# A two-layer decoder step on one core: low parts of the normalized input moved from VectorE to GpSimd, weight splits and norm sums reordered

## The chip, the cores and the metric

One Trainium2 chip, one core of it. The metric is the time of one execution in microseconds, as the device reports it; the median of several runs is given. The engines are called as in the profile: PE (TensorE), DVE (VectorE), ACT (ScalarE), POOL (GpSimd), SP (the engine whose queue issues most loads).

## The reference

One inference step of two layers, on a prompt of 256 tokens and 8 sampled tokens (264 columns in all), width 1024, float32. Layer 0 mixes tokens by a gated short convolution, layer 1 by block-sparse attention with 8 heads of 128. Each layer has one input projection to 4096 columns, a mixer, a gate and one output projection, and ends in a layer norm of the residual:

```
q, k, v, z = jnp.split(x @ w_in, 4, axis=-1)          # layer 1
yp = (o.reshape(Bp, Tp, D_MODEL) * jax.nn.silu(z)) @ w_out_attn[j]
xp = _layernorm(DN_ALPHA * xp + yp, ln_g[i], ln_b[i])  # both layers
```

So the normalized output of layer 0, called x1 here, is the input of layer 1's projection. That is the place of the change.

## The kernel before

**Products.** Activations lie feature by token: 8 blocks of 128 features, each 264 columns wide. A weight is taken in slabs: slab n holds 128 output features as 8 blocks of 128x128. Slabs 0 to 31 are layer 0's input projection, 32 to 39 its output projection, 40 to 71 layer 1's input projection (q in 40 to 47, then k, v, z) and 72 to 79 the output projection. To keep float32 accuracy at the speed of a rounded format, each operand is split into a rounded high part and a low part, which is the difference; per block k, `mm` (L136 to L138) issues three products: high by high, low weight by high, high weight by low. A slab is 24 products into one PSUM accumulator. There are three accumulators under the tag "acc", used in turn, so slab n writes the one that slab n - 3 wrote and has to wait until that has been read.

**Splits of weights.** `load` (L112) brings a slab by a DMA from SP, `hi` (L124) rounds it on ACT, `lo` (L129) takes the difference on DVE. Where each is issued is written by hand: `hi_slot` and `lo_slot` give the slab during which it is issued, and behind `lo` of a slab the load of the slab four places on is issued, into the buffer that has just come free.

**Order.** All engines run their instructions in program order. Before the products of slab n, `begin(n)` runs the work hooked to n by `at(n, phase, ...)`, phase by phase: dma, pe, s0, hi, lo, s1a, s1b, s1, s1c, and then, by `split_late`, hi3 and lo3. Within a phase the order is that of registration. For slabs 40 and 41 this is written out by hand (from L1027 on), with `split_late` called apart.

**The norm between the layers.** In slabs 33 to 39, `evac` adds the projection to the residual in `xf`, `square` squares it on ACT, and `sums` adds values and squares over the eight blocks on POOL, into the tiles sr and q (264 wide). `last_sums` adds block 7 on DVE. `stats_mm` (L335) multiplies the two with a column of 1/1024 (of -1/1024 for the mean), each in four products of 66 tokens that go to four groups of 32 partitions (L341); it is issued behind blocks 0 to 3 of slab 40. `stats` then gets the negative mean and the reciprocal of the deviation: a copy and a square on ACT (L349, L350), a subtraction on DVE (L351), a root on ACT (L352), a reciprocal on DVE (L353). Sixteen small copies spread these to the tile nr (L357): five on DVE, four on POOL, seven on ACT, those of ACT behind the rounding of slab 45.

**Slabs 40 to 46** don't wait for the norm: they multiply the residual, scaled by the norm's gain, and are mended afterwards. `u_evac` (L580 to L583) does this for one slab on DVE: a copy of two columns, a product that adds the accumulator (L582, its last reader) and a product with the reciprocal of the deviation (L583). `u_fin` adds the bias on ACT (L586) and POOL copies the 8 sampled columns (L587).

**Slabs 47 to 71** multiply x1. `x1_norm` subtracts the mean and scales, in two passes on DVE (L839, L840). `x1_affine` applies gain and bias on ACT (L844) and rounds (L845, the high part). `x1_low` (L848) takes the low part on DVE. These are hooked two blocks at a time: norms of blocks 0 and 1 in slab 41, 2 and 3 in 42, 4 and 5 in 43, 6 and 7 in 44; low parts 0 and 1 in slab 43, 2 and 3 in 45, 4 to 7 in 46.

**In the middle of slab 47**, behind its block 3, PE takes 64 products of the sampled tokens' scores (L745). They read the tile zq, which DVE fills in slab 46 (shuffle and rotation from L622 on, then L736) from POOL's copies of heads 0 to 3.

The lines around the change:

```
for n, norm, low in ((42, (2, 3), ()), (43, (4, 5), (0, 1)), (44, (6, 7), ()),
                     (45, (), (2, 3)), (46, (), (4, 5, 6, 7))):
    for m in norm:
        at(n, "s1", x1_norm, m)
        at(n, "s1", x1_affine, m)
    for m in low:
        at(n, "s1", x1_low, m)
```

Of the kernel before, what the change touches and what calls it, by code (L numbers as in the profile page):

```python
# [10 lines left out]
F32 = mybir.dt.float32  # L11
# [3 lines left out]
AF = mybir.ActivationFunctionType  # L15
ALU = mybir.AluOpType
# [5 lines left out]
N = T + B  # L22
# [27 lines left out]
def build(tc, a):  # L50
    nc = tc.nc
    pe, act, dve, pool, sp = nc.tensor, nc.scalar, nc.vector, nc.gpsimd, nc.sync

    with ExitStack() as top:
# [7 lines left out]
        def acc_full():  # L62
            return psp.tile([128, 512], F32, tag="acc", bufs=3, name="acc")

        def acc_tile():
            return acc_full()[:, 0:N + 2]

        def att_tile(nm):
            return psp.tile([128, 512], F32, tag="att", bufs=3, name=nm)
# [20 lines left out]
        xf = cp.tile([128, NB, N], F32, name="xf")  # L90
# [3 lines left out]
        pair = [[t[:, :, 4:N + 6] for t in ts] for ts in rows_of]  # L94
# [36 lines left out]
        def mm(acc, n, mv, ks, first=True, last=True):  # L131
            mh, ml = mv
            w = acc.shape[-1]
            for k in ks:
                wh, wl = his[n][:, k, :], los[n][:, k, :]
                pe.matmul(acc, wh, mh[:, k, 0:w], start=first and k == ks[0], stop=False)  # L136
                pe.matmul(acc, wl, mh[:, k, 0:w], start=False, stop=False)  # L137
                pe.matmul(acc, wh, ml[:, k, 0:w], start=False, stop=last and k == ks[-1])  # L138
# [4 lines left out]
        def at(n, phase, f, *args):  # L143
            hooks.setdefault((n, phase), []).append(lambda: f(*args))

        def run(n, phase):
            for f in hooks.pop((n, phase), []):
# [2 lines left out]
        hi_slot = {4: 3, 5: 3, 6: 3, 7: 4, 8: 4, 9: 5, 10: 5, 11: 6, 38: 33, 39: 34, 40: 22, 41: 24, 42: 26,  # L150
                   43: 36, 44: 37, 45: 40, 46: 41, 47: 43, 48: 45, 49: 46, 50: 47, 51: 48, 52: 48, 53: 49,
                   54: 51, 55: 52, 56: 53, 57: 53, 58: 54, 65: 61, 66: 62, 67: 63, 68: 63, 78: 74}
        lo_slot = {4: 3, 5: 3, 6: 3, 7: 4, 8: 5, 9: 5, 45: 40, 46: 42, 47: 44, 51: 49, 52: 49,
                   53: 50, 54: 51, 55: 52, 56: 53, 57: 54, 58: 54, 61: 58, 62: 59, 63: 60, 64: 61, 65: 61, 66: 62, 67: 63, 39: 34}

        order = []
# [4 lines left out]
        for i, n in enumerate(order):  # L161
            hs = hi_slot.get(n, n - 5)
            late = "3" if 45 <= n < 50 else ""
            at(hs, "hi" + late, hi, n)
            ls = lo_slot.get(n, hs + 1)
            if n in (61, 62, 65):
                late = "4"
            elif ls in (56, 57, 58):
                late = "3"
            elif n == 46:  # L170
                late = ""
            at(ls, "lo" + late, lo, n)
            if i + 4 < len(order):
                at(ls, "lo" + late, load, order[i + 4])

        def begin(n, end=True):
            for ph in ("dma", "pe", "s0", "hi", "lo", "s1a", "s1b", "s1", "s1c"):
                run(n, ph)
            if end:
                split_late(n)  # L180
# [75 lines left out]
        onem = cp.tile([128, 2, 32], F32, name="onem")  # L256
# [28 lines left out]
        G = N // 4  # L285
# [4 lines left out]
        class Norm:  # L290
# [23 lines left out]

            def square(self, m):
                if m == 0:
                    self.q = self.t("q")
                    act.activation(self.q, xf[:, 0], AF.Square)
                    return
                self.sq[m] = lnp.tile([128, N], F32, tag="sqm", bufs=2, name=f"sqm{m}{self.gi}")  # L320
                act.activation(self.sq[m], xf[:, m], AF.Square)

            def sums(self, m):
                if m == 1:
                    self.sr = self.t("sr")
                    pool.tensor_tensor(self.sr, xf[:, 0], xf[:, 1], ALU.add)
                else:
                    pool.tensor_tensor(self.sr, self.sr, xf[:, m], ALU.add)
                pool.tensor_tensor(self.q, self.q, self.sq[m], ALU.add)
# [3 lines left out]
                dve.tensor_add(self.q, self.q, self.sq[7])  # L333

            def stats_mm(self):  # L335
                self.mean = att_tile("ln0")
                self.e2 = att_tile("ln1")

                def acc(p, w, src, first, last):
                    for j in range(4):  # L340
                        pe.matmul(p[32 * j:32 * j + 32, 0:G], w, src[:, G * j:G * j + G],  # L341
                                  start=first, stop=last)
                acc(self.mean, onem[:, 0], self.sr, True, True)
                acc(self.e2, onem[:, 1], self.q, True, True)

            def stats(self):
                self.st = self.t("st", 2 * G)
                var = self.t("var", G)
                act.copy(self.st[:, 0:G], self.mean[:, 0:G])  # L349
                act.activation(var, self.mean[:, 0:G], AF.Square)  # L350
                dve.tensor_sub(var, self.e2[:, 0:G], var)  # L351
                act.activation(var, var, AF.Sqrt, bias=epst)  # L352
                dve.reciprocal(self.st[:, G:2 * G], var)  # L353

# [136 lines left out]
        for n in range(4, 32):  # L491
# [3 lines left out]
            acc = acc_tile()[:, 0:N]  # L495
# [39 lines left out]
        with tc.tile_pool(name="l1", bufs=1) as p1, ExitStack() as late_pool:  # L535
            x1 = pair[1]
# [305 lines left out]
            def x1_affine(m):  # L842
                c = xf[:, m]
                act.activation(c, c, AF.Identity, bias=ln.bcol(m), scale=ln.gcol(m))  # L844
                act.copy(x1[0][:, m, 0:N], c)  # L845

            def x1_low(m):
                dve.tensor_sub(x1[1][:, m, 0:N], xf[:, m], x1[0].bitcast(F32)[:, m, 0:N])  # L848

            S = 40  # L850

# [34 lines left out]
            for h in range(8):  # L886
                n = S + 16 + h
# [138 lines left out]

            ac2 = [acc_tile() for _ in range(2)]  # L1027
            begin(40, False)
            mm(ac2[0], 40, pair[0], range(0, 4), last=False)
            ln.stats_mm()  # L1030
            ln.stats()
            ln.nr = lnp.tile([128, 4, 2 * G], F32, name="nr")
# [2 lines left out]
            ln.spread(pool.tensor_copy, [(j, 1) for j in range(4)])  # L1035
            split_late(40)
            ln.spread(act.copy, [(j, 3) for j in range(4)] + [(j, 2) for j in range(3)])
            mm(ac2[0], 40, pair[0], range(4, 7), first=False, last=False)
            begin(41, False)
            mm(ac2[1], 41, pair[0], range(0, 3), last=False)  # L1040
            for m in (0, 1):
# [1 line left out]
            split_late(41)  # L1043
            for m in (0, 1):
                x1_affine(m)
            mm(ac2[1], 41, pair[0], range(3, 7), first=False, last=False)
            for i in range(2):
                mm(ac2[i], 40 + i, pair[0], range(7, 8), first=False)
                at(42, "s0", u_evac, i, ac2[i])
                at(42, "s1", u_fin, i)  # L1050
            for n, norm, low in ((42, (2, 3), ()), (43, (4, 5), (0, 1)), (44, (6, 7), ()),
                                 (45, (), (2, 3)), (46, (), (4, 5, 6, 7))):
                for m in norm:
                    at(n, "s1", x1_norm, m)
                    at(n, "s1", x1_affine, m)
                for m in low:
                    at(n, "s1", x1_low, m)
            for i in range(2, 32):
                n = S + i
                begin(n)  # L1060
                mv = pair[0] if i < NU else x1
                acc = acc_tile()
                if i >= NU:
                    acc = acc[:, 0:N]
# [43 lines left out]
            last = [acc_full(), att_tile("c1b")]  # L1108
# [11 lines left out]
            for k in range(8):  # L1120
                for c in range(2):
                    for j in range(4):
                        pe.matmul(ps[32 * j:32 * j + 32], gs[:, c, k, :],  # L1123
                                  wide(raws, k)[:, 256 * j + 128 * c:256 * j + 128 * c + 128],
                                  start=k == 0 and c == 0, stop=False)
# [93 lines left out]
```

## Time and profile before

| | |
|---|---|
| median of 3 runs | 276.52 us (276.19 to 276.76) |
| the profiled execution | 276.77 us, of which the span of the program 275.0 us |
| PE busy | 270.2 us (98%) |
| DVE busy | 203.5 us (74%) |
| ACT busy | 170.6 us (62%) |
| POOL busy | 64.9 us (24%) |
| granted clock of PE | 1.0 |

How to read it: the profile is of one execution. Times are from the start of its span. In a timeline, a row gives the start and the duration in us, the engine, the line of the kernel (L129), the operation, the tile written and those read, the shapes and how many instructions are merged; in brackets the engine's idle time before it, and what ended that. Shares of busy time are means over the whole span; the place of the change is the stretch from 120 to 150 us. Records of one engine can overlap a little, since an instruction starts before the one ahead has fully ended.

### The profile page before, as it was taken

To read this page: it belongs to the slowest core of one execution; us is meant where nothing else is said; L and a number is where in the kernel's file an instruction comes from. 1 tells how busy PE (TensorE), PEld (TensorE's weight loads), DVE (VectorE), ACT (ScalarE), POOL (GpSimd) and SP (SyncE) were. 2 spreads that over 40 slices of the span, in tenths; PEclk is the share of its full clock that TensorE was granted. 3 is DMA by queue.
4 is the path that set the end of the run, shared out by engine and by line. 5 is a ranking of instruction groups with operands and counts; after the bars stand their busy time and mean duration, and the time that the engine had idled before them with its cause. 6 is when DMAs were issued, how large, how long until landed. Compare 5 with 4: busy or idle time off the path is not lost.

```text
span 275.0 us, 6282 instructions
## 1 busy us (share of the span) xinstructions
PE 270.2 (98%) x2307; PEld 254.7 (93%) x2307; DVE 203.5 (74%) x415; ACT 170.6 (62%) x348; POOL 64.9 (24%) x129
## 2 busy tenths in 40 slices
PE   8999999999999999999999999999999999999994
PEld 5999999999999999999999997999959996998883
DVE  3888966655775857979999839799857484994745
ACT  4786554453655628549686665888746854599302
POOL 1121532020110101961312365721100030000122
PEclk9999999999999999999999999999999999999999
DMA  7976879999785875142223999997989955782012
GB/s 245 401 274 223 281 286 333 396 360 377 245 266 197 283 227 189 56 147 76 80 76 99 343 401 357 337 393 233 354 308 348 391 183 174 219 272 75 1 76 88
DMA packets 24336, 66.48 MB, mean 242 GB/s; under 512 B 3058, under 2 KB 6898, under 8 KB 24178
## 3 DMA queue, kind: packets, MB, share of 16 engines
q1 hardware_dynamic: 23874, 65.69, 68.0%
q8 instruction: 18, 0.29, 0.4%
q10 hardware_dynamic: 432, 0.39, 0.4%
q14 instruction: 12, 0.10, 0.1%
HBM read 61.67 MB, written 3.35 MB: 236 GB/s over the span
## 4 chain that ended last, share of the span: by engine, by line
PE 98%; ACT 0%; DVE 0%; issue 0%
PE acc L136 24%; PE acc L137 24%; PE acc L138 24%; PE c L1010 4%; PE acc L472 3%; PE sd L745 3%; PE dps L796 3%; PE c1b L1010 2%; PE acc L1010 2%; PE acc L475 1%; PE so L1123 1%; PE warmp L80 1%; PE s L679 1%; PE o L717 1%; PE pt L707 1%; PE s L677 1%
## 5 line engine op out<-in xcount | busy, mean ns | idle before, releaser
L124 ACT CAST hi<-raw 128x1024 fp32r<-128x1024 f32 x76 | 79.0, 1049 | 34.3 <-DMA raw<-w 15.7
L129 DVE TENSOR_TENSOR lo<-raw,hi 128x1024 fp32r<-128x1024 f32 x76 | 92.7, 1230 | 7.1 <-ACT hi L124 3.9
L136 PE MATMUL acc<-m0h,hi 128*128 128x264 f32 (+1 forms) x280 | 79.4, 283 | 0.0
L138 PE MATMUL acc<-m0l,hi 128*128 128x264 f32 (+1 forms) x280 | 79.2, 283 | 0.0
L137 PE MATMUL acc<-m0h,lo 128*128 128x264 f32 (+1 forms) x280 | 79.2, 283 | 0.0
L136 PE MATMUL acc<-m1h,hi 128*128 128x264 f32 x264 | 76.4, 289 | 0.0
L138 PE MATMUL acc<-m1l,hi 128*128 128x264 f32 x264 | 74.6, 282 | 0.0
L137 PE MATMUL acc<-m1h,lo 128*128 128x264 f32 x264 | 74.5, 282 | 0.0
L137 PEld LDWEIGHTS acc<-m0h,lo 128*128 128x128 f32 x280 | 52.8, 189 | 0.0
L136 PEld LDWEIGHTS acc<-m0h,hi 128*128 128x128 f32 x280 | 52.6, 188 | 0.1
L138 PEld LDWEIGHTS acc<-m0l,hi 128*128 128x128 f32 x280 | 52.7, 188 | 0.0
L136 PEld LDWEIGHTS acc<-m1h,hi 128*128 128x128 f32 x264 | 49.6, 188 | 1.7 <-issue 0.8
L137 PEld LDWEIGHTS acc<-m1h,lo 128*128 128x128 f32 x264 | 49.8, 189 | 0.0
L138 PEld LDWEIGHTS acc<-m1l,hi 128*128 128x128 f32 x264 | 49.5, 188 | 0.0
L428 POOL COPY uo<-up 128x10 f32<-128x10 f32 x8 | 9.0, 1122 | 64.3 <-DVE up L427 58.5
L635 POOL COPY vs<-vh 128x8 f32<-128x8 f32 x8 | 3.0, 375 | 33.1 <-ACT vh L634 33.1
L688 DVE CUSTOM_DVE_ANT_0 P<-s,cst 128x128 f32<-128x128 f32 (+1 forms) x16 | 5.1, 355 | 6.2 <-PE s L679 6.2
L436 DVE SCALAR_TENSOR_TENSOR t<-up,cst,t 128x256 f32<-128x256 f32 x8 | 3.9, 483 | 6.9 <-ACT t L435 6.9
L825 POOL COPY zs<-z 128x8 f32<-128x8 f32 x8 | 3.0, 378 | 24.4 <-ACT z L824 24.4
L824 ACT ACTIVATE z<-acc 128x264 f32<-128x264 f32 x8 | 3.1, 386 | 9.0 <-PE acc L138 9.0
L952 ACT ACTIVATE zq<-raw 128x1024 f32<-128x1024 f32 x8 | 8.5, 1061 | 0.1
L427 DVE TENSOR_TENSOR up<-acc,h 128x264 f32<-128x264 f32 x8 | 3.4, 430 | 6.9 <-PE acc L138 6.9
(226 smaller groups left out, 446.5 us busy)
## 6 DMA issues: line engine op xcount, KB each, us to landing
raw<-w SPq DMA_DIRECT2D x76, 512.0 KB, 4.5
kv<-kc SPq DMA_DIRECT2D x32, 256.0 KB, 6.2
kv<-vc SPq DMA_DIRECT2D x16, 512.0 KB, 6.4
first<-first SPq DMA_DIRECT2D x6, 388.0 KB, 7.1
v_o<-vh SPq DMA_DIRECT2D x8, 132.0 KB, 5.5
xf<-kall SPq DMA_DIRECT2D x16, 64.0 KB, 2.6
kall<-gb SPq DMA_DIRECT2D x1, 1024.0 KB, 6.1
k_o<-kall SPq DMA_DIRECT2D x6, 132.0 KB, 5.4
```

Of the source, the lines that this page charges most:

```text
L124: act.copy(his[n][sl], raws[n][sl])
L129: dve.tensor_sub(los[n][sl], raws[n][sl], his[n].bitcast(F32)[sl])
L136: pe.matmul(acc, wh, mh[:, k, 0:w], start=first and k == ks[0], stop=False)
L137: pe.matmul(acc, wl, mh[:, k, 0:w], start=False, stop=False)
L138: pe.matmul(acc, wh, ml[:, k, 0:w], start=False, stop=last and k == ks[-1])
L428: pool.tensor_copy(uo[:, f], up[:, T:N + 2])
L472: pe.matmul(accs[s], wh, (mh, ml)[c], start=k == 0 and c == 0, stop=False)
L688: dve.tensor_tensor_reduce(out=P[sl], in0=s_ps[h][sl], in1=mask[sl], scale=-SCALE, scalar=3e38, op0=ALU.add, op1=ALU.min, accum_out=mx[:, ...
L745: pe.matmul(s[32 * j:32 * j + 16, 0:256], zq[:, o:o + 16], kt, start=step == 0 and i == 0, stop=step == 3 and i == 3)
L796: pe.matmul(dps[0][32 * j:32 * j + 32, 512 * c:512 * c + 512], pm[b2][pg][:, j, :], kv_tiles[step, j][:, 512 * c:512 * c + 512], start=ste ...
L952: act.activation(od, wide(raws, k), AF.Copy, accum_out=wsum[:, k:k + 1])
L1010: pe.matmul(acc, g[m][:, k, t], wide(d, k)[:, c0:c1], start=k == 0 and i == 0, stop=k == 7 and i == 2)
```

## The change

It has four parts, all between slab 40 and slab 47.

- **Norm sums.** The sums sr and q become the two halves of one tile, and `stats_mm` makes four products of 2 x 66 columns instead of twice four of 66. They go behind block 4 of slab 40 instead of block 3. The mean comes out positive and ACT turns its sign in L349.
- **Splits.** `lo` of slab 45 moves from slot 40 (behind the DVE copies of nr) to slot 42, and `lo` of slab 46 from slot 42 to slot 43; both come behind the `u_evac` of their slot. The loads of slabs 49 and 50 move with them.
- **Low parts.** `x1_low` runs on POOL instead of DVE, and earlier: blocks 0 and 1 behind their rounding in slab 41, then 2 and 3 in slab 43, 4 and 5 in 44, 6 and 7 in 45.
- **Order on ACT.** In slab 44, gain and rounding of blocks 6 and 7 go to phase s1c, behind `u_fin` of slab 43.

```diff
-        lo_slot = {4: 3, 5: 3, 6: 3, 7: 4, 8: 5, 9: 5, 45: 40, 46: 42, 47: 44, 51: 49, 52: 49,
+        lo_slot = {4: 3, 5: 3, 6: 3, 7: 4, 8: 5, 9: 5, 45: 42, 46: 43, 47: 44, 51: 49, 52: 49,
...
-            elif n == 46:
+            elif n in (45, 46):
                 late = ""
...
             def stats_mm(self):
-                self.mean = att_tile("ln0")
-                self.e2 = att_tile("ln1")
-
-                def acc(p, w, src, first, last):
-                    for j in range(4):
-                        pe.matmul(p[32 * j:32 * j + 32, 0:G], w, src[:, G * j:G * j + G],
-                                  start=first, stop=last)
-                acc(self.mean, onem[:, 0], self.sr, True, True)
-                acc(self.e2, onem[:, 1], self.q, True, True)
+                p = att_tile("ln1")[:, 0:2 * G]
+                for j in range(4):
+                    pe.matmul(p[32 * j:32 * j + 32], onem[:, 1], self.both[:, :, G * j:G * j + G],
+                              start=True, stop=True)
+                self.mean, self.e2 = p[:, 0:G], p[:, G:2 * G]
...
-                act.copy(self.st[:, 0:G], self.mean[:, 0:G])
-                act.activation(var, self.mean[:, 0:G], AF.Square)
-                dve.tensor_sub(var, self.e2[:, 0:G], var)
+                act.activation(self.st[:, 0:G], self.mean, AF.Copy, scale=-1.0)
+                act.activation(var, self.mean, AF.Square)
+                dve.tensor_sub(var, self.e2, var)
...
             def x1_low(m):
-                dve.tensor_sub(x1[1][:, m, 0:N], xf[:, m], x1[0].bitcast(F32)[:, m, 0:N])
+                pool.tensor_tensor(x1[1][:, m, 0:N], xf[:, m], x1[0].bitcast(F32)[:, m, 0:N], ALU.subtract)
...
-            mm(ac2[0], 40, pair[0], range(0, 4), last=False)
+            mm(ac2[0], 40, pair[0], range(0, 5), last=False)
             ln.stats_mm()
...
-            mm(ac2[0], 40, pair[0], range(4, 7), first=False, last=False)
+            mm(ac2[0], 40, pair[0], range(5, 7), first=False, last=False)
...
             for m in (0, 1):
                 x1_affine(m)
+                x1_low(m)
...
-            for n, norm, low in ((42, (2, 3), ()), (43, (4, 5), (0, 1)), (44, (6, 7), ()),
-                                 (45, (), (2, 3)), (46, (), (4, 5, 6, 7))):
+            for n, norm, low in ((42, (2, 3), ()), (43, (4, 5), (2, 3)), (44, (6, 7), (4, 5)),
+                                 (45, (), (6, 7))):
                 for m in norm:
                     at(n, "s1", x1_norm, m)
-                    at(n, "s1", x1_affine, m)
+                    at(n, "s1c" if n == 44 else "s1", x1_affine, m)
```

More of the change, by code (lines that the diff above doesn't have):

```diff
@@ L316, in square @@
                 if m == 0:
-                    self.q = self.t("q")
+                    self.both = self.t("both", 2 * N).rearrange("p (c n) -> p c n", c=2)
+                    self.sr, self.q = self.both[:, 0], self.both[:, 1]
                     act.activation(self.q, xf[:, 0], AF.Square)
@@ L324, in sums @@
                 if m == 1:
-                    self.sr = self.t("sr")
                     pool.tensor_tensor(self.sr, xf[:, 0], xf[:, 1], ALU.add)
```

## The prediction

> **What bounds the kernel now.** I read the page first, then PE's waits, then the timeline engine by engine from 117 to 144 us.
>
> ```profile
> span 275.0 us, 6282 instructions
> ...
> PE 98%; ACT 0%; DVE 0%; issue 0%
> ```
>
> ```profile
> PE warmp L80 <- PEq L1200: 0.8, 1, 0.8
> PE st L1139 <- ACT zq L1136: 0.5, 1, 0.5
> PE sd L745 <- issue: 0.2, 1, 0.2
> ```
>
> The chain that ends last is PE nearly throughout, and the second view (us in total, times, longest) says that PE waits for other engines almost nowhere: at its start, at its end, and once for 0.2 us ahead of the decode scores at L745. What the change can win is therefore small: that wait, and PE's own work on the norm sums. What it can lose is not bounded in this way; it depends on how close the other engines run behind PE. The stretch in question, PE alone:
>
> ```profile
> 122.18 0.28 PE L138 MATMUL acc<-m0l,hi 128*128 128x266 f32 x1
> 122.39 0.32 PE L341 MATMUL ln<-sr,onem 128*32 128x66 f32 x8
> 122.55 0.32 PE L341 MATMUL ln<-q,onem 128*32 128x66 f32 x8
> 122.80 0.39 PE L136 MATMUL acc<-m0h,hi 128*128 128x266 f32 x1
> ...
> 142.11 0.28 PE L136 MATMUL acc<-m1h,hi 128*128 128x264 f32 x1
> ...
> 143.43 0.28 PE L138 MATMUL acc<-m1l,hi 128*128 128x264 f32 x1
> 143.86 4.00 PE L745 MATMUL sd<-kv,zq 128*16 128x256 f32 x64 [0.16 <-issue]
> ```
>
> Slab 47, the first that reads the normalized x1, starts at 142.11. Now DVE in the same stretch:
>
> ```profile
> 125.95 1.23 DVE L129 TENSOR_TENSOR lo<-raw,hi 128x1024 fp32r<-128x1024 f32 x1
> 127.09 0.43 DVE L839 TENSOR_TENSOR xf<-xf,nr 128x264 f32<-128x264 f32 x1
> ...
> 136.35 0.77 DVE L848 TENSOR_TENSOR m1l<-xf,m1h 128x264 fp32r<-128x264 f32 x2
> 137.04 0.15 DVE L580 COPY uv<-acc 128x2 f32<-128x2 f32 x1
> ...
> 139.82 1.22 DVE L129 TENSOR_TENSOR lo<-raw,hi 128x1024 fp32r<-128x1024 f32 x1
> 140.96 0.15 DVE L580 COPY uv<-acc 128x2 f32<-128x2 f32 x1
> 141.15 0.49 DVE L582 SCALAR_TENSOR_TENSOR t<-nr,uv,acc 128x264 f32<-128x264 f32 x1
> 141.67 0.43 DVE L583 TENSOR_TENSOR t<-t,nr 128x264 f32<-128x264 f32 x1
> 142.02 0.77 DVE L848 TENSOR_TENSOR m1l<-xf,m1h 128x264 fp32r<-128x264 f32 x2
> 142.72 0.18 DVE L622 STREAM_SHUFFLE qsr<-qs 32x32 f32<-32x32 f32 x1
> ...
> 143.47 0.27 DVE L736 COPY zq<-qs 128x16 f32<-128x16 f32 x2
> ```
>
> No row here carries an idle time: DVE is full from 125.95 on. Two of its results are nearly late. The product of L582 at 141.15 is the last reader of slab 44's accumulator, and with three accumulators that is the one slab 47 writes: it ends at 141.64, and PE starts at 142.11, so the slack is 0.47 us. And L736 ends at 143.74 while PE is ready for L745 some 0.2 us after 143.43: that is the 0.2 us wait. **DVE is the second bound of this stretch, with half a microsecond to spare.**
>
> **Part 1: the sums in one tile, three products later.** (The step is k = 4 of slab 40, three products of 0.12 us.) On PE the statistics now take 122.80 - 122.18 less one product's 0.12, that is 0.50 us. Four products of twice the width go where two groups of four went. The second group starts 0.16 after the first; a group twice as wide should need about 0.09 more than a narrow one (an estimate: between nothing and that 0.16). PE gains 0.07, between 0 and 0.16. The order costs something too, on the other engines:
>
> ```profile
> 122.78 0.22 ACT L349 COPY st<-ln 128x66 f32<-128x66 f32 x1 [0.42 <-PE ln L341]
> ...
> 124.78 2.17 ACT L357 COPY nr<-st 32x132 f32<-32x132 f32 x7
> ...
> 128.67 0.41 ACT L845 CAST m1h<-xf 128x264 fp32r<-128x264 f32 x1
> ```
>
> L349 reads the mean at 122.78, after the first group alone. Now it waits for the one wide group, which starts 0.37 later: I take 0.37 + 0.09 = 0.46 (0.37 to 0.53). Everything to the copies of L357 is a chain behind it, so they end at 127.41 instead of 126.95. DVE's first normalization (L839) reads them. It stood at 127.09, behind the split of 45; now it starts at 127.45: **+0.36**. DVE idles for the 1.1 us that the split used to fill. The scale of -1 on L349 costs nothing that a row shows.
>
> **Part 2: order on DVE up to 141.15.** The split of 45 (1.14 from its start to the next, 139.82 to 140.96) moves from ahead of the first normalization to behind the evacuations of slabs 40 and 41, and that of 46 goes behind the evacuation of 42. The list from L839 to the evacuation of slab 44 thus holds one split more (+1.14), and loses the two low parts of 136.35 (137.04 - 136.35 = 0.69): **+0.45**. The splits themselves are wanted by slabs 45 and 46, several us later. Each carries a weight load on SP:
>
> ```profile
> 127.20 14.19 SPq L112 DMA_DIRECT2D raw<-w  x3
> ```
>
> ```profile
> raw<-w SPq DMA_DIRECT2D x76, 512.0 KB, 4.5
> ```
>
> SP issues nothing else there. The load of 49 goes out about 133 instead of 127.2, and lands 4.5 later; its rounding is due in slot 46, after 142. The load of 50 is about 138, its rounding still later. Nothing.
>
> **Part 3: the low parts on GpSimd.** In the trace POOL subtracts nothing in this stretch, but a little earlier it adds tiles of the same 128x264, beside DVE. DVE, then POOL:
>
> ```profile
> 117.08 1.21 DVE L129 TENSOR_TENSOR lo<-raw,hi 128x1024 fp32r<-128x1024 f32 x1
> 118.22 0.98 DVE L510 SCALAR_TENSOR_TENSOR m0l<-xf,cst,m0h 128x264 fp32r<-128x264 f32 x1
> 119.13 0.41 DVE L300 SCALAR_TENSOR_TENSOR xf<-xf,acc 128x264 f32<-128x264 f32 x1
> ...
> 122.41 0.89 DVE L510 SCALAR_TENSOR_TENSOR m0l<-xf,cst,m0h 128x264 fp32r<-128x264 f32 x2
> ```
>
> ```profile
> 117.30 1.61 POOL L328 TENSOR_TENSOR sr<-sr,xf 128x264 f32<-128x264 f32 x1 [0.20 <-DVE xf L300]
> 118.88 0.95 POOL L329 TENSOR_TENSOR q<-q,sqm 128x264 f32<-128x264 f32 x1
> 119.78 0.76 POOL L328 TENSOR_TENSOR sr<-sr,xf 128x264 f32<-128x264 f32 x1
> ```
>
> Alone, a POOL sum takes 0.76 (the last row). The one of 117.30 meets the split L129 and takes 1.61: it ends at 118.91, 0.62 after the split's end at 118.29. DVE's L510 of 118.22, two of which take 0.89 when POOL rests, now takes 0.98 by itself: it ends at 119.20, 0.29 after POOL's end. POOL's next ends at 119.83, again 0.63 after that. They take turns, and neither runs while the other does. L300, which reads its second operand from PSUM, keeps its 0.41 in the middle of a POOL sum. So what collides is a DVE pass with two operands in SBUF and a POOL pass that reads SBUF. Normalization (L839, L840), the last product of an evacuation (L583) and every split (L129) are such passes; L580 and L582 are not.
>
> The Trainium skill states this in "SBUF — State Buffer", section "Who interferes with whom": the pair of ports that VectorE and GpSimd share is an exclusive lock, held for the whole instruction, and a VectorE instruction with two SBUF inputs contends with a GpSimd instruction that reads SBUF. The trace agrees on who blocks whom, but has 0.62 of the 0.76 as the time held; held whole, six low parts would cost at most 6 x 0.14 = 0.84 more, and the forecast would be about 279.9 (an estimate).
>
> Low part by low part, with 0.62 for POOL from grant, 0.29 for a blocked 264-wide DVE pass after POOL's end, and ACT's rounding as the earliest start. Low 0: rounding ends at 129.08 + 0.46 = 129.54, POOL runs 129.60 to 130.36. DVE is then in the evacuation of slab 40, begun at 129.08; its last product (L583) starts 0.71 later at 129.79, is blocked, and ends at 130.65 instead of 130.22: +0.43. Carried on in the same way: low 1 (130.56 to 131.32) falls under L580 and L582, +0.05. Low 2 (134.85 to 135.61) blocks the last product of slab 42's evacuation, +0.26. Low 3 (from 135.81) takes the ports just before the split of 46, +0.61 (the other way round POOL comes second and blocks the normalization behind, about as much). Lows 4 and 5 are queued on POOL behind slab 42's small copy, run from 141.26 and 142.13, and block the last normalization by 0.45 and the split of 47 by 0.56. Sum **+2.36**. From both sides: nothing, were there no lock; 6 x 0.62 = 3.7 if every one met DVE head on. I keep 2.36, since the rows above match it to a few hundredths. Lows 6 and 7 come after; slab 47 wants them only behind L745.
>
> ACT's order (blocks 6 and 7 behind the finish of slab 43) lets POOL's copy for L622 go early; in the trace of before it wasn't what L622 waited for, so it gains nothing, and it keeps POOL's queue from making L736 later still.
>
> **The sum.** 0.36 + 0.45 + 2.36 = 3.17. L582 for slab 44 ends at 141.64 + 3.17 = 144.81, and slab 47 starts there instead of at 142.11: +2.7 (of this some 0.9 shows already as a wait of slab 46 for slab 43's evacuation). Then slab 47 needs 1.32 and 0.2 to L745; L736 ends about 146.25, when PE is just ready, so the 0.2 wait goes. Net **+2.5 us**. PE's 0.07 is swallowed by the wait. Behind L745 lie 4.00 us of scores in which DVE, relieved of four low parts, catches up, and PE has no wait there that could absorb the delay. The profiled execution took 276.77 (its span 275.0); it would become 279.3. That execution is 0.25 above the median of the runs shown, 276.52, so I forecast **279.0**.
>
> **Rivals.**
> *No lock for these passes.* L300 shows that not every DVE pass minds POOL. If a subtraction beside DVE cost nothing, DVE would be 0.81 late against 0.47 of slack: slab 47 starts 0.34 late, the 0.2 wait goes, +0.13: 276.65, not slower by anything that can be told. It decides at 0.81 - 0.47: under it, the low parts cost nothing. Against it: L510's 0.98. Chance 0.14. "Perfetto Trace Analysis", section "Optimizing Scalar/DVE Operations" of the Trainium skill says that with a saturated DVE, moving some work to GPSIMD may make sense, though between those two it might not help.
> *A gain.* Were the chain of L349 not later either, PE would win its 0.07 and the 0.2: 276.25. No view shows more to win. Chance 0.04.
> *Half the collisions.* POOL's passes slip under L580, L582 and idle time: 1.2 instead of 2.36, so +1.3, 277.8. Chance 0.10.
> *More than forecast.* PE stands still for 0.9 and 1.8 us, and may resume at the speed it had at its start:
>
> ```profile
> 4.25 1.25 PE L472 MATMUL acc<-m0h,hi 128*128 128x264 f32 x4
> ```
>
> Four products there lie 0.22 apart instead of 0.12. Slab 47's first twelve at that pace add 1.2: 280.2. Chance 0.07. "TensorE: Matmul & The Clock Gate", section "What's actually happening" of the Trainium skill, has the clock fall back after an idle window of about 3.4 us; by that, pauses of this length would not do it.
> *The change doesn't do what it says:* DVE doesn't get freer, since each low part leaves 0.34 and brings back up to 0.6 as waiting. That is the forecast itself, and what it is likeliest to be wrong about is the size.
>
> **How the numbers follow.** Forecast (+1.7 to +3.3, that is 278.2 to 279.8) 0.65, and the other chances above. A measurement of this kernel tells about 0.2%, 0.55 us, from no change. Slower: 0.65 + 0.10 + 0.07 = 0.82; within: 0.14; faster: 0.04. The unknown price is that of a POOL subtraction beside DVE; the range takes in its bounds, from 276.6 (none) to 280.4 (every low part head on: 0.81 + 3.7 - 0.47 - 0.2 is +3.8), and this holds the slow restart too.
>
> **What would show it.** Right: PE waits on L582's evacuations, some 0.9 us ahead of slab 46 and 1.8 ahead of slab 47, and none ahead of L745; normalizations, L583 and splits that take 0.7 to 1.8 beside POOL's subtractions, and subtractions of 0.76 to 1.0; the first normalization near 127.45 behind 1 us of idle DVE. Wrong: splits of 1.22 and products of 0.43 throughout beside POOL's subtractions, or slab 47 starting by 142.6.

## The result, and the profile after

| | before | after |
|---|---|---|
| median | 276.36 us (276.08 to 276.76, 6 runs) | 279.38 us (279.05 to 279.83, 6 runs) |
| profiled execution | 276.77 us | 279.11 us |
| its span | 275.0 us | 277.1 us |

The ratio is 1.0110 (95% interval 1.0096 to 1.0123): the change makes the kernel slower by 3.0 us. Line numbers of after are smaller by 3 in the norm sums and by 4 from the statistics on: L835 and L836 normalize, L576 to L579 evacuate, L844 takes a low part, L741 are the scores.

The page of after, the span and the chain that ended last:

```profile
span 277.1 us, 6271 instructions
...
PE 91%; DVE 6%; ACT 2%; issue 1%; DVEq 0%
```

PE had 98% of the chain and has 91%; DVE has come in with 6%. PE's waits (us in total, times, longest):

```profile
PE acc L136 <- DVE t L578: 2.4, 2, 1.7
PE warmp L80 <- PEq L1197: 0.8, 1, 0.8
PE st L1136 <- ACT zq L1133: 0.5, 1, 0.5
```

Two waits for L578, the last reader of an accumulator, are new, and the 0.2 us ahead of the scores is gone. PE's timeline shows where they stand:

```profile
120.38 0.28 PE L136 MATMUL acc<-m0h,hi 128*128 128x266 f32 x1
...
122.14 0.29 PE L138 MATMUL acc<-m0l,hi 128*128 128x266 f32 x1
122.36 0.43 PE L338 MATMUL ln<-both,onem 128*32 128x132 f32 x8
122.72 0.39 PE L136 MATMUL acc<-m0h,hi 128*128 128x266 f32 x1
...
138.57 0.28 PE L138 MATMUL acc<-m0l,hi 128*128 128x266 f32 x1
139.61 0.36 PE L136 MATMUL acc<-m0h,hi 128*128 128x266 f32 x1 [0.75 <-DVE t L578]
...
142.50 0.28 PE L138 MATMUL acc<-m0l,hi 128*128 128x266 f32 x1
144.44 0.36 PE L136 MATMUL acc<-m1h,hi 128*128 128x264 f32 x1 [1.65 <-DVE t L578]
144.63 0.28 PE L137 MATMUL acc<-m1h,lo 128*128 128x264 f32 x1
...
145.84 0.28 PE L138 MATMUL acc<-m1l,hi 128*128 128x264 f32 x1
146.05 1.22 PE L741 MATMUL sd<-kv,zq 128*16 128x256 f32 x15
```

The first row is the start of slab 40; the last holds 15 of the 64 score products, since this view ends at 146.9. Slab 46 starts 1.04 behind the last product of slab 45 instead of the usual 0.12, and slab 47 1.94 behind that of slab 46: together 2.74 lost. The scores follow slab 47's last product after 0.21.

For comparing the two traces one thing has to be taken out. In before, slab 40 starts here:

```profile
120.80 0.28 PE L136 MATMUL acc<-m0h,hi 128*128 128x266 f32 x1
```

That is 0.42 later than in after, though hardly anything is changed ahead of it. Over the ten traces of this study it starts between 119.99 and 120.81. All of this spread arises in the first 12 us: from the fifth group of products of L475 (L471 in after), which starts at 12.14 in before and at 11.73 in after, it is 108.65 or 108.66 us to slab 40 in each of the ten. I therefore count from slab 40's start. To the end of the span this is 275.0 - 120.80 = 154.2 before and 277.1 - 120.38 = 156.7 after, or +2.55 by the trace's three decimals. The start of slab 47 is at 144.44 - 120.38 = 24.06 instead of 142.11 - 120.80 = 21.31: **+2.75**.

DVE, then POOL, in the same stretch of after:

```profile
127.05 0.43 DVE L835 TENSOR_TENSOR xf<-xf,nr 128x264 f32<-128x264 f32 x1 [1.12 <-ACT nr L353]
...
129.40 0.83 DVE L579 TENSOR_TENSOR t<-t,nr 128x264 f32<-128x264 f32 x1
...
130.86 0.46 DVE L579 TENSOR_TENSOR t<-t,nr 128x264 f32<-128x264 f32 x1
...
134.77 0.70 DVE L579 TENSOR_TENSOR t<-t,nr 128x264 f32<-128x264 f32 x1
135.40 1.21 DVE L129 TENSOR_TENSOR lo<-raw,hi 128x1024 fp32r<-128x1024 f32 x1
136.53 0.99 DVE L835 TENSOR_TENSOR xf<-xf,nr 128x264 f32<-128x264 f32 x1
...
141.12 0.88 DVE L836 TENSOR_TENSOR xf<-xf,nr 128x264 f32<-128x264 f32 x1
141.92 1.78 DVE L129 TENSOR_TENSOR lo<-raw,hi 128x1024 fp32r<-128x1024 f32 x1
...
143.80 0.49 DVE L578 SCALAR_TENSOR_TENSOR t<-nr,uv,acc 128x264 f32<-128x264 f32 x1
...
144.90 0.51 DVE L619 TENSOR_SCALAR qs<-qs,cst 32x32 f32<-32x32 f32 x1
...
145.71 0.27 DVE L732 COPY zq<-qs 128x16 f32<-128x16 f32 x2
```

```profile
129.18 1.67 POOL L844 TENSOR_TENSOR m1l<-xf,m1h 128x264 fp32r<-128x264 f32 x2 [3.33 <-ACT m1h L841]
...
134.43 0.75 POOL L844 TENSOR_TENSOR m1l<-xf,m1h 128x264 fp32r<-128x264 f32 x1 [0.20 <-ACT m1h L841]
135.38 1.85 POOL L844 TENSOR_TENSOR m1l<-xf,m1h 128x264 fp32r<-128x264 f32 x1 [0.20 <-ACT m1h L841]
...
140.75 1.86 POOL L844 TENSOR_TENSOR m1l<-xf,m1h 128x264 fp32r<-128x264 f32 x2
```

Read the two against each other. Low part 3 on POOL begins at 135.38, a moment before the split at 135.40, and comes second: the split keeps its 1.21 and ends at 136.61; the low part ends at 137.23, 0.62 later; and the normalization queued behind, L835, ends at 137.52, 0.29 after that, having taken 0.99 instead of 0.43. Lows 4 and 5, the last row, do the same with L836 (0.88) and the split of 47 (1.78 instead of 1.22). Each time the three ends follow one another. A pass alone takes 0.76 on POOL and 0.43 or 1.22 on DVE; one that waited ends 0.62, or 0.29 and 1.09, after the other's end. So but for about 0.14 us of each, these passes don't run while the other does.

### The profile page after: what moved, and what is told of

Its sections match the earlier page's. It is cut to its first block, busy times and chain, and to the rows that moved or that the text cites. A ratio compares the mean times of both kernels' runs of the same rounds, so it can differ in the third digit from the quotient of the medians.

```text
span 277.1 us, 6271 instructions
## 1 busy us (share of the span) xinstructions
PE 270.0 (97%) x2299; PEld 254.0 (92%) x2299; DVE 203.8 (74%) x407; ACT 170.4 (61%) x348; POOL 70.0 (25%) x137
## 4 chain that ended last, share of the span: by engine, by line
PE 91%; DVE 6%; ACT 2%; issue 1%; DVEq 0%
PE acc L136 22%; PE acc L138 21%; PE acc L137 21%; PE c L1006 4%; PE acc L468 3%; PE sd L741 3%; PE dps L792 3%; PE c1b L1006 2%; PE acc L1006 2%; DVE lo L129 1%; PE acc L471 1%; PE so L1120 1%; PE warmp L80 1%; DVE xf L835 1%; PE s L675 1%; PE o L713 1%
## 5 line engine op out<-in xcount | busy, mean ns | idle before, releaser
L124 ACT CAST hi<-raw 128x1024 fp32r<-128x1024 f32 x76 | 79.0, 1049 | 31.7 <-DMA raw<-w 16.3
L424 POOL COPY uo<-up 128x10 f32<-128x10 f32 x8 | 8.0, 1003 | 65.2 <-DVE up L423 58.1
L844 POOL TENSOR_TENSOR m1l<-xf,m1h 128x264 fp32r<-128x264 f32 x8 | 7.7, 966 | 3.9 <-ACT m1h L841 3.7
```

The lines of the kernel that those rows point to most:

```text
L124: act.copy(his[n][sl], raws[n][sl])
L424: pool.tensor_copy(uo[:, f], up[:, T:N + 2])
L844: pool.tensor_tensor(x1[1][:, m, 0:N], xf[:, m], x1[0].bitcast(F32)[:, m, 0:N], ALU.subtract)
```

## The experiments

The theory is that of the forecast. Three causes add up on DVE's list, and DVE's lateness reaches PE through the accumulator that slab 47 reuses. These are the later statistics (part 1), one split more on the list (part 2) and POOL's subtractions in the way of DVE's passes with two operands in SBUF (part 3). The rivals give the loss to fewer of them, or to POOL's place in the order and not to the ports. The first four kernels of the table were timed beside runs of before with a median of 276.56, the other four beside 276.31. The last column is the time from slab 40's start to the end of the span, against that of before.

| kernel | median us | ratio (95%) | us | trace, us |
|---|---|---|---|---|
| after without part 3 | 278.06 | 1.0057 (1.0039 to 1.0074) | +1.50 | +1.50 |
| part 3 alone | 277.88 | 1.0052 (1.0035 to 1.0070) | +1.32 | +1.40 |
| part 2 alone | 277.65 | 1.0044 (1.0028 to 1.0061) | +1.09 | +1.09 |
| part 1 alone | 277.00 | 1.0016 (1.0005 to 1.0028) | +0.44 | +0.41 |
| after, POOL only writes | 276.65 | 1.0017 (1.0007 to 1.0027) | +0.34 | +0.11 |
| after once more | 279.18 | 1.0098 (1.0083 to 1.0112) | +2.87 | +2.54 |
| before, one product deferred | 275.96 | 0.9989 (0.9977 to 1.0000) | -0.35 | -0.46 |
| the same, wide sums | 276.04 | 0.9989 (0.9979 to 0.9999) | -0.27 | -0.27 |

**After without part 3.** The low parts go back to DVE, at the places they had:

```
-                pool.tensor_tensor(x1[1][:, m, 0:N], xf[:, m], x1[0].bitcast(F32)[:, m, 0:N], ALU.subtract)
+                dve.tensor_sub(x1[1][:, m, 0:N], xf[:, m], x1[0].bitcast(F32)[:, m, 0:N])
...
-            for n, norm, low in ((42, (2, 3), ()), (43, (4, 5), (2, 3)), (44, (6, 7), (4, 5)),
-                                 (45, (), (6, 7))):
+            for n, norm, low in ((42, (2, 3), ()), (43, (4, 5), (0, 1)), (44, (6, 7), ()),
+                                 (45, (), (2, 3)), (46, (), (4, 5, 6, 7))):
```

> The changed kernel with the low parts back on DVE at their old places; splits, norm sums and the order on ACT stay changed. Theory (POOL's subtractions and DVE's passes with two SBUF operands exclude each other): the six collisions of 2.4 us are gone, but the two low parts of 0.34 each stand on DVE again ahead of slab 44's evacuation, two more ahead of the score tile, and DVE's 1.1 us of idle time and the additional split remain: +1.4 us against the kernel before, and no split above 1.45 us. Rival (POOL's subtractions cost DVE nothing, the reordered splits and sums cost all): as slow as the changed kernel or slower, +3.0 or more.

It came to +1.50. All five splits between 119 and 150 us are of one length (durations as shortest, median, longest):

```profile
L129 DVE TENSOR_TENSOR lo<-raw,hi x5: 1216/1218/1222, 131.0 to 149.6; 128x1024 fp32r<-128x1024 f32 x5
```

So half of the loss is there with no subtraction on POOL, and with the subtractions gone no split is lengthened and no normalization takes more than 0.46. Its PE waits need care:

```profile
PE acc L136 <- ACT m1h L841: 0.7, 1, 0.7
...
PE sd L741 <- ACT hi L124: 0.4, 1, 0.4
PE acc L136 <- DVE t L578: 0.2, 1, 0.2
```

The view names ACT twice. But L841 ends at 142.91 and DVE's L578 at 142.89, so the view alone can't tell the two apart. The distances do: slab 47 starts 0.15 behind the end of L578 here, as in the other traces in which it waits (0.14 or 0.15), while its distance from L841 differs (0.43 in after). The scores start 0.13 behind the end of L732, as in before, and 0.28 behind that of L124. So I take L578 and L732 for what PE waited for.

**Part 3 alone.** Before, with POOL's subtraction, `x1_low` behind `x1_affine` in slab 41 and after's table of hooks.

```
+                pool.tensor_tensor(x1[1][:, m, 0:N], xf[:, m], x1[0].bitcast(F32)[:, m, 0:N], ALU.subtract)
...
                 x1_affine(m)
+                x1_low(m)
```

> The kernel before with part 3 alone: low parts on POOL, at the new places. Theory: five to six collisions push slab 44's evacuation from 0.47 us of slack to about 1.1 us late, +1.35 us; normalizations, last products and splits of DVE that meet a subtraction take 0.7 to 1.8 us. Rival: DVE is relieved of two low parts ahead of the evacuation, nothing is late, and the 0.2 us wait ahead of the scores goes: -0.1 to -0.2 us.

It came to +1.32, although DVE has eight passes less. DVE's timeline:

```profile
139.75 0.88 DVE L840 TENSOR_TENSOR xf<-xf,nr 128x264 f32<-128x264 f32 x1
140.55 1.78 DVE L129 TENSOR_TENSOR lo<-raw,hi 128x1024 fp32r<-128x1024 f32 x1
142.25 0.14 DVE L580 COPY uv<-acc 128x2 f32<-128x2 f32 x1
142.43 0.49 DVE L582 SCALAR_TENSOR_TENSOR t<-nr,uv,acc 128x264 f32<-128x264 f32 x1
142.96 0.95 DVE L583 TENSOR_TENSOR t<-t,nr 128x264 f32<-128x264 f32 x1
```

0.88, 1.78 and 0.95 are again the lengths of a pass that waited for POOL, with the other two parts undone; L580 and L582, which read PSUM, keep theirs. Slab 40 starts at 120.66 in this trace, so L582 is at 21.77 behind it instead of 20.35, 1.42 later.

**Part 2 alone.**

```
-        lo_slot = {4: 3, 5: 3, 6: 3, 7: 4, 8: 5, 9: 5, 45: 40, 46: 42, 47: 44, 51: 49, 52: 49,
+        lo_slot = {4: 3, 5: 3, 6: 3, 7: 4, 8: 5, 9: 5, 45: 42, 46: 43, 47: 44, 51: 49, 52: 49,
...
-            elif n == 46:
+            elif n in (45, 46):
```

> The kernel before with part 2 alone: splits of 45 and 46 behind evacuations. Theory: the copies on ACT end at 126.95 as before, so DVE idles about 1.05 us in place of the split of 45 and has one split more in the list up to slab 44's evacuation: that evacuation comes 1.05 us later against 0.47 of slack, and the score tile 1.05 later: +0.9 to +1.0 us. Rival (the whole loss is the collisions): under +0.2 us.

It came to +1.09. The first normalization shows what the split of 45 had filled:

```profile
126.81 0.43 DVE L839 TENSOR_TENSOR xf<-xf,nr 128x264 f32<-128x264 f32 x1 [1.12 <-ACT nr L357]
...
142.01 0.49 DVE L582 SCALAR_TENSOR_TENSOR t<-nr,uv,acc 128x264 f32<-128x264 f32 x1
...
144.34 0.27 DVE L736 COPY zq<-qs 128x16 f32<-128x16 f32 x2
```

In before DVE worked at the split until then. Here it idles for 1.12 us, and the 1.14 of the split comes back further down: slab 40 starts at 120.57 in this trace, so L582 is at 21.44 behind it instead of 141.15 - 120.80 = 20.35, 1.09 later. At PE this shows in two places:

```profile
PE acc L136 <- ACT q L586: 0.6, 1, 0.6
...
PE sd L745 <- ACT hi L124: 0.4, 1, 0.4
```

The view names ACT here too, but slab 47 starts 0.15 behind the end of L582, and the scores 0.13 behind that of L736. Against before, slab 47 is 0.77 later and the scores are 1.10 later. L736 fills the score tile, and that tile has no slack at all: PE waited for it in before already.

**Part 1 alone.** Before with the sums in one tile, four products of 132, behind block 4 (the edits of L314 to L353 and of the two ranges in slab 40).

> The kernel before with part 1 alone: one tile for the sums, products of double width behind block 4. Theory as first put: everything behind the mean comes 0.46 us later, so does the first normalization; slab 44's evacuation uses up its slack, the score tile is 0.4 later: +0.35 us, less 0.07 on PE. Rival: the trace of the changed kernel shows the statistics hardly later than before (the copies of nr start at 124.47 against 124.45), so the chain costs nothing and PE gains 0.05: -0.05 to 0.

It came to +0.44. The rival had read absolute times, in which the copies of after are no later than those of before (124.47 against 124.45); but after's slab 40 starts 0.42 earlier. Here slab 40 starts at 120.63. Its first normalization, the second row, behind the split of 45:

```profile
126.21 1.23 DVE L129 TENSOR_TENSOR lo<-raw,hi 128x1024 fp32r<-128x1024 f32 x1
127.35 0.43 DVE L835 TENSOR_TENSOR xf<-xf,nr 128x264 f32<-128x264 f32 x1
```

Counted from slab 40, that is 127.35 - 120.63 = 6.72, where before has 127.09 - 120.80 = 6.29: 0.43 later. The scores start 0.44 later, so the lateness comes out whole: again the score tile, without slack, passes it on, and neither PE's small gain on the sums nor the slack at L582 takes anything off.

**Do the three add?** On DVE's list they nearly do: L582 for slab 44 is 1.42, 1.09 and 0.43 later in the three variants, 2.94 in all, and 3.07 in after. At PE the sum of the medians, 1.32 + 1.09 + 0.44 = 2.85, equals the whole change (2.87 beside the second set of runs), but in part by luck. Each part alone makes the scores wait, and there almost nothing is taken off. In after the score tile is in time: from the start of L582 to the end of L736 DVE needs 2.18 instead of 2.58, since two low parts are gone from there (in part 3 alone L583 is held up in their place, and it is 2.69). So slab 47 decides, and its slack is taken off. The traces from slab 40 on show the difference: 1.40 + 1.09 + 0.41 = 2.90 for the parts, 2.55 for the whole. The order on ACT, the fourth part, was not run alone. In after DVE goes into the shuffle of L618 without idle time, so it didn't wait there for POOL's copy, and a gain by that order is not shown.

**After, POOL only writes.**

```
             def x1_low(m):
-                pool.tensor_tensor(x1[1][:, m, 0:N], xf[:, m], x1[0].bitcast(F32)[:, m, 0:N], ALU.subtract)
+                pool.memset(x1[1].bitcast(F32)[:, m, 0:N], 0.0)
+                pool.memset(pad, 0.0)
```

> The changed kernel with each subtraction of POOL replaced by two memsets (264 and 512 wide, together about as long as the subtraction): the low parts of x1 are left out. POOL is as busy at the same places, but reads nothing from SBUF. Theory (what collides is a POOL pass that reads SBUF with a DVE pass that has two operands there): no DVE pass is lengthened, DVE is 0.8 us late against 0.47 of slack, +0.1 to +0.4 us against the kernel before. Rival (POOL's queue or its activity as such delays the stretch): as slow as the changed kernel, about +3 us.

This kernel leaves out the low parts of x1. It came to +0.34: of the 3.0 us all but about a tenth is gone, with POOL writing at the same places of its order, for about as long per block (0.31 and 0.52; the writes don't wait for the roundings, so that those of blocks 0 and 1 run earlier). POOL and DVE of this kernel:

```profile
139.09 0.31 POOL L846 MEMSET m1l<- 128x264 f32 x1
139.34 0.52 POOL L847 MEMSET pad<- 128x512 f32 x1
139.81 0.31 POOL L846 MEMSET m1l<- 128x264 f32 x1
140.08 0.52 POOL L847 MEMSET pad<- 128x512 f32 x1
```

```profile
139.02 0.43 DVE L835 TENSOR_TENSOR xf<-xf,nr 128x264 f32<-128x264 f32 x1
139.48 0.43 DVE L836 TENSOR_TENSOR xf<-xf,nr 128x264 f32<-128x264 f32 x1
139.83 1.22 DVE L129 TENSOR_TENSOR lo<-raw,hi 128x1024 fp32r<-128x1024 f32 x1
...
141.15 0.49 DVE L578 SCALAR_TENSOR_TENSOR t<-nr,uv,acc 128x264 f32<-128x264 f32 x1
```

The same passes of DVE, with POOL writing all the while, take 0.43 and 1.22. So it is not POOL's being busy, nor its writing, that blocks them; what the subtraction does besides is to read SBUF. This is what the Trainium skill says in "SBUF — State Buffer", section "Who interferes with whom": a VectorE instruction with two SBUF inputs contends with a GpSimd instruction that reads SBUF, not with one that only writes it. This variant also is the no-lock rival as an experiment. That put DVE 0.81 late, and here, with slab 40 at 119.99, L578 is at 21.16 behind it instead of 20.35: 0.81. It was priced at +0.13; the median has +0.34, the trace +0.11.

**After once more,** unchanged, beside the last three variants.

> The changed kernel once more, beside the others on one chip. Its trace, counted from slab 40, has 2.5 us more than the trace before; its runs have 3.0 more. If the difference is the spread of the start ahead of slab 40 between two single traces, the runs here lie 2.5 to 3.0 above the kernel before and a second trace counted from slab 40 gives 2.5 again; if the collisions fall differently from run to run, the second trace has other waits ahead of slabs 46 and 47 than 0.9 and 1.8.

It came to +2.87, +2.54 in the trace, and its waits for L578 are again 2.4 us in two. Low part 3 comes second behind the split once more.

**Before, one product deferred.** If DVE's list is what makes the scores wait, something not urgent should be taken off it at the right place. The last product of slab 44's evacuation (L583) is wanted much later than zq; it goes behind zq's copies.

```
+                if h != 4:
+                    u_rs(h)
...
+                    if h == 4:
+                        at(S + 6, "s0", u_rs, h)
+                        at(S + 6, "s0", u_fin, h)
```

> The kernel before with one move: the last product of slab 44's evacuation (0.35 of DVE, not a reader of the accumulator) comes behind the filling of the score tile, with its finish. Theory (DVE's list ahead of the score tile is what PE waits for): the tile is ready 0.35 earlier, the 0.2 us wait goes, -0.2 us. Rival (the wait is POOL's copy of slab 43's columns, which ends at 142.16): -0.2 as well but only to 142.2 for the shuffle; or no change if something else is late.

It came to -0.35 (-0.46 in the trace). PE's timeline:

```profile
143.44 0.28 PE L138 MATMUL acc<-m1l,hi 128*128 128x264 f32 x1
143.65 3.77 PE L749 MATMUL sd<-kv,zq 128*16 128x256 f32 x64
147.35 0.39 PE L136 MATMUL acc<-m1h,hi 128*128 128x264 f32 x1
```

The scores follow after 0.21 instead of before's 0.43: the wait that the whole change could win is won by moving one product. This is the 0.2 that was expected; the rest of the trace's 0.46 comes from the scores themselves (last section).

**The same, with the wide sums** behind block 3, where the narrow ones stood.

> The same move, and the sums in one tile with products of double width, but at their old place behind block 3. Theory: PE gains another 0.05, the chain behind the mean comes about 0.15 to 0.25 later, which the slack of 0.47 and the move's 0.35 take up: -0.2 to -0.25 us. Rival (any lateness behind the mean is paid in full): 0 to +0.1.

-0.27, with an interval that overlaps the other's: whether the wide sums help can't be told from the times; in its trace, from slab 40 on, this version is 0.19 behind the other. Both versions are faster than before by about 0.1%, which is less than the 0.2% that I took as told apart; the first one's interval ends at 1.0000.

## Why the prediction was right, point by point

**The bound.** That DVE is less than half a microsecond ahead of PE's need was the reading that carried everything, and the experiments bear it out in the main: what made DVE's list longer came out at PE. One thing the reading left out is that the half microsecond holds at L582 alone. The score tile has nothing to spare, and part 1, whose 0.43 is less than the 0.47, came out in full at the scores.

**Part 1.** On PE the statistics took 122.72 - 122.14 = 0.58 instead of 0.62: a gain of 0.04, forecast 0.07, and swallowed as forecast. The first normalization is at 127.05 - 120.38 = 6.67 instead of 6.29: +0.38, forecast +0.36, with the 1.12 us of idle DVE in its row (forecast 1.1).

**Part 2.** The split of 1.14 more on the list, forecast from its row, is the 1.09 at L582 when part 2 is done alone. The other half of the forecast's 0.45, two low parts less, belongs with part 3. Together with part 1 it shows where POOL only writes: 0.36 + 0.45 = 0.81 was forecast, and L578 is 0.81 later there.

**Part 3.** By the rows above, against 0.43 and 1.22: 0.40 + 0.03 + 0.27 + 0.56 + 0.45 + 0.56 = 2.27. By L578 for slab 44: 143.80 - 120.38 = 23.42 instead of 141.15 - 120.80 = 20.35, +3.07, less 0.38 and 0.45, leaves 2.24; less the 0.81 of the variant in which POOL only writes, it leaves 2.26. The forecast was 2.36. The term that differed most was low 3 (0.56, not 0.61), where POOL came second behind the split of 46, the other way round that the forecast named. The time held was again 0.62 and not the whole 0.76. It is these rows that decide against the estimate by the Trainium skill's rule that the ports are held for the whole instruction. Its 279.9 is above all six runs, but only just (279.83 at most).

**At PE.** Slab 47 starts 2.75 later (forecast 2.7). Here two small errors of the forecast met. It took 0.47 as slack, the distance from L582's end to slab 47; but PE follows L578's end (143.80 + 0.49 = 144.29) only after 0.15, at 144.44. The slack was 0.32, and 3.07 - 0.32 = 2.75. Part 2 alone agrees: 1.09 - 0.32 = 0.77, and its slab 47 starts 0.77 later; part 3 alone has 1.42 - 0.32 = 1.10, and starts 1.10 later. So the collisions were over-estimated by about 0.1 and the slack by 0.15. Behind that, slab 47's first product is 0.19 ahead of the second instead of 0.12, and the wait ahead of the scores loses 0.22 (0.21 instead of 0.43): 2.75 + 0.07 - 0.22 = 2.60 at L741, and +2.55 at the end. The forecast was +2.5.

**The rivals.** No lock: out by the lengths of the rows, and shown from the other side by POOL's writes. Half the collisions: 2.24 were met instead of 1.2. A slow restart, as at the program's start: the twelve products from 144.44 to 145.84 are 0.12 apart from the second on, where the start had 0.22. "TensorE: Matmul & The Clock Gate", section "What's actually happening" of the Trainium skill, has the clock fall back only after an idle window of about 3.4 us; pauses of 1.0 and 1.9 us agree. A gain: the 0.2 us wait did go, but at the price of the two others.

**What stays open.** The medians differ by 3.02 and 2.87, the traces from slab 40 on by 2.55 and 2.54. The 2.55 lies inside the second ratio's interval (+2.3 to +3.1) and just under the first one's (+2.65 to +3.4). The forecast took the profiled execution's distance to the median of before, 0.25, for after as well. If after also loses 0.3 us ahead of slab 40, it is in the first 12 us, where the change touches nothing: from there to slab 40 all ten traces agree to 0.01. Whether the two kernels differ there on average, or only single executions do, these runs don't settle.

## What to carry to other kernels

When the bounding engine waits for nothing, look for the engine whose results arrive last before their use, and measure that slack for each such result: here 0.32 us at L582 (the distance less the 0.15 that PE needs to follow) and none at the score tile. What the change did to DVE beyond that came out at PE. Moving a pass of 0.34 us from DVE to POOL gains nothing where both read SBUF: DVE got back 0.4 to 0.56 of waiting for four of the six. Of the time that it saved, only two passes (0.69) had stood ahead of L582; two more stood ahead of the score tile alone, and four behind both. A late result is made earlier by moving what is not urgent behind it on the same engine: that was a few lines, and the median is 0.35 lower, with an interval that just reaches no change.

## What the runs showed that was not expected

- L619, a pass of DVE with a single tensor operand of 32x32, took 0.51 beside POOL's subtraction, 0.33 beside POOL's memset and 0.23 alone. It was not among the passes that the forecast let collide. The same section of "SBUF — State Buffer" says that such a pass can enter a mode that uses both pairs of ports and then contends; the rows agree, and no run tries it by itself.
- With one product deferred, the 64 score products took 143.65 to 147.35, 3.70 us, instead of before's 143.86 to 147.79, 3.93. That is 0.23 on top of the wait itself. The five traces in which PE waits ahead of the scores have 3.92 or 3.93; those in which it doesn't have 3.70, 3.71, 3.78 and, in the two of after, 3.86 and 3.87. The cause is open.
- Slab 40 starts up to 0.8 us apart in the ten traces, which are of nine kernels, and the spans of before's own executions go from 274.0 to 275.1. So two spans alone don't tell a change of half a microsecond.
